# Two loads for expert 0's x, and b2 loaded behind the entry, in a mixture-of-experts kernel

## The chip, the cores and the metric

The kernel runs on one core of a Trainium2 chip. The metric is device time in microseconds (us); the median of three runs counts. All durations below come from one profiled execution.

## The reference

```python
# x (8, 256, 512), w1 (8, 512, 2048), w2 (8, 2048, 512), b1 (8, 2048), b2 (8, 512), all float32
h = np.matmul(x, w1) + b1[:, np.newaxis, :]
h = np.maximum(h, 0)
return (np.matmul(h, w2) + b2[:, np.newaxis, :]).astype(np.float32)
```

Eight experts, each with 256 rows of x: two matrix products, a bias and a ReLU between them, a bias behind. The weights are 64 MB of float32 in HBM, x and the output 4 MB each.

## The kernel before, in words

**Tiling.** All products are done in fp16 with float32 sums. An expert's first product makes h transposed, 128 of the 2048 hidden columns at a time: 16 groups j of four matmuls (128 x 128 weights against 128 x 256 of x transposed), summed in one of four PSUM tiles `ph`; ScalarE (ACT) adds b1 and applies the ReLU on the way into `hT` (L106). The second product sums over the 16 groups into `po`, 512 columns wide, in two halves of 128 rows, and begins with a matmul of one row of ones against b2 (L303). The results go over ACT or VectorE (DVE) into float32 tiles and from there to HBM.

**Steps.** TensorE (PE) runs a hardware loop of 11 steps (L268). In step s it does the first product of expert s (s < 8) and the second of expert s - 3. Before the first product it waits for `w1_in` and `xT_full` (L271, L272), before each half of the second for `w2_in` (L313). SyncE (SP) turns the completion of a weight load into `w1_in` or `w2_in`: in step s it waits for the load's semaphore `s_w1[s % 3]` (L144) and counts `w1_in` up; step 0 has no wait of its own.

**Weights.** Three buffers each for w1 and w2. GpSimd (POOL) issues the loads, which convert float32 to fp16 on the way (L163, L171): w1 of expert 0 ahead of everything (L352), w1 of experts 1 and 2 at once in `run_gpsimd`, and each later one when a buffer is free. w1 of expert 3 waits for `ph_full` = 16 (L162), that is until PE has done all 16 groups of expert 0. Each of these loads has 128 packets of 16 KB, 8 on each of the 16 DMA engines. All loads issued by POOL go through one DMA queue (q0, software), all issued by SP through another (q1, hardware).

**The start.** `first_loads` (L340) issues on SP: x of expert 0 and x of expert 1 (each 128 partitions of two rows, 4 KB in one piece, into `pair`), b1 (32 rows of 2 KB), and x of experts 2 and 3 together ("x2", 128 partitions of 8 KB, into `outg`). On POOL it issues w1 of expert 0 and then b2 (8 KB of fp16, one partition, 16 packets of 512 bytes). `first_turns` (L354) then makes an identity (POOL memsets, a DVE transpose at L360, ACT copies at L363), casts x of experts 0 and 1 to fp16 on ACT (L365), transposes them on PE (L372) and copies the result into `xT` on ACT (L373); DVE transposes b1 (L375), ahead of L360 in its order. A framework schedules these and inserts the waits.

**The entry.** Everything else stands in one critical section (L381) with semaphores written out by hand. On entry PE, ACT, DVE and SP each wait for every load and every engine of the start: the four loads of SP, w1 of expert 0, b2, and the last copies. POOL alone goes in without waiting and takes the same waits only at L180, after it has issued w1 of experts 1 and 2. Behind the entry ACT first counts `xT_full`, `ph_free` and the others up (L191 to L194) and casts x2 (L195), and DVE transposes it (L222).

**The end.** The groups' results leave on q0 (L187), the last two experts' on q1 (L155, L389).

Of the kernel before, what the change touches and what calls it, by code (L numbers as in the profile page):

```python
# [10 lines left out]
def kernel(  # L11
# [9 lines left out]
    nc = tc.nc  # L21
# [6 lines left out]
    nTB = T // P  # L28
# [5 lines left out]
    NW = 3  # L34
# [13 lines left out]
    def sb(name, shape, dt=fp16):  # L48
        return nc.alloc_sbuf_tensor(name, shape, dt).ap()

    w1_f = sb("w1sb", [P, NW * nKC * M + nJ])
    w1_sb = w1_f[:, 0 : NW * nKC * M].rearrange("p (n kc m) -> p n kc m", n=NW, kc=nKC)
# [6 lines left out]
    b2_sb = sb("b2sb", [1, E * H])  # L59
# [10 lines left out]
    def sem(name):  # L70
        return nc.alloc_semaphore(name)

    s_x = sem("s_x")
    s_w1 = [sem(f"s_w1_{i}") for i in range(NW)]
# [51 lines left out]
    def out_of(first, n):  # L126
        return out[first : first + n].rearrange("e (p r) h -> (e p) r h", r=n * nTB)

    x32 = {e: pair[e] for e in range(2)}
    x32[2] = grouped[0][:, 0 : FIRST[2] * nTB, :]  # L130

    def w1_of(e):
        return w1[e].rearrange("(p kc) m -> p kc m", kc=nKC)

    def x_of(first):
        n = FIRST[first]
        return x[first : first + n].rearrange("e (p r) h -> (e p) r h", r=n * nTB)

    def run_sync():
        s = nc.sync  # L140
        for step in range(E + LAG):
            if step < E:
                if step:
                    s.wait_ge(s_w1[step % NW], 16 * ((step + NW - 1) // NW))  # L144
                s.sem_inc(w1_in, 1)  # L145
            if step >= LAG:
                e = step - LAG
                for h in range(2):
                    if (e, h) in s_w2:
                        s.wait_ge(s_w2[e, h], 16)  # L150
                    s.sem_inc(w2_in, nQ // 2)  # L151
                    if e == E - 1 and h == 0:
                        s.wait_ge(po_free_a, E)
                        s.wait_ge(po_free_d, E)
                        s.dma_start(out=out_of(E - 2, 1), in_=pair[0]).then_inc(s_out[E - 2], 16)  # L155

    def run_gpsimd():
        g = nc.gpsimd

        def load_w1(e):  # L160
            if e >= NW:
                g.wait_ge(ph_full, nJ * (e - NW + 1))  # L162
            g.dma_start(out=w1_sb[:, e % NW], in_=w1_of(e)).then_inc(s_w1[e % NW], 16)  # L163

        def load_w2(e):
            if e >= NW:
                g.wait_ge(po_full, ENDS * (e - NW + 1))
            src = w2[e].rearrange("(p j) h -> p j h", j=nJ)
            cuts = (0, CUT[e], nJ) if e in CUT else (0, nJ)
            for h, (lo, hi) in enumerate(zip(cuts, cuts[1:])):  # L170
                g.dma_start(  # L171
                    out=w2_sb[:, e % NW, lo:hi], in_=src[:, lo:hi]).then_inc(s_w2[e, h], 16)

        for step in range(1, E + LAG):
            if step < E:
                if step == 4:
                    g.dma_start(out=x16[step], in_=x_of(step)).then_inc(s_x, 16)
                load_w1(step)
            if step == NW - 1:
                tc.wait_critical_data_deps()  # L180
            if step >= LAG:
                load_w2(step - LAG)
        g.wait_ge(s_w2[E - 1, 0], 16)
        for first in sorted(GROUPS, reverse=True):
            done = 1 + first + GROUPS[first]
            g.wait_ge(po_free_a, done)
            g.dma_start(out=out_of(first, GROUPS[first]), in_=grouped[first]).then_inc(  # L187
                s_out[first], 16)
# [150 lines left out]

    def first_loads():  # L340
        for to, rows in (
            (x32[0], x_of(0)),
            (x32[1], x_of(1)),
            (b1_rows, b1.rearrange("e (b i) -> (e b) i", b=nB)),
            (x32[2], x_of(2)),
        ):
            tc.keep_in_program_order(nc.sync.dma_start(out=to, in_=rows))  # L347
        for to, rows in (
            (w1_sb[:, 0], w1_of(0)),
            (b2_sb, b2.rearrange("e h -> (e h)").rearrange("(o f) -> o f", o=1)),  # L350
        ):
            tc.keep_in_program_order(nc.gpsimd.dma_start(out=to, in_=rows))  # L352

    def first_turns():  # L354
        g, v, a, t = nc.gpsimd, nc.vector, nc.scalar, nc.tensor
# [18 lines left out]
        for b in range(nB):  # L374
            v.transpose(  # L375
                out=b1T[b * B : (b + 1) * B, nB - 1 - b : nB - 1 - b + nJ * B],
                in_=b1_rows.rearrange("r (i j) -> r j i", j=nJ))

    first_loads()
    first_turns()  # L380
    with tc.tile_critical(sync_engine=mybir.EngineType.Pool, no_gpsimd_drain=True):  # L381
        run_gpsimd()
        run_sync()
        run_scalar()
        run_vector()
        run_tensor()
        nc.sync.wait_ge(po_free_a, 1 + E)
        nc.sync.wait_ge(po_free_d, 1 + E)
# [38 lines left out]
```

## Time and profile before

| | |
|---|---|
| median of 3 runs | 180.66 us (180.63 to 181.15) |
| profiled execution, its own time | 180.8 us |
| its span, first to last instruction | 179.0 us |
| mean granted TensorE clock | 0.975 |
| busy: PE, ACT, DVE, POOL | 73%, 48%, 21%, 7% of the span |
| DMA packets | 3825, 40.98 MB as counted at the destination |
| HBM read and written | 71.39 MB and 4.19 MB |

How to read the lines below. A line of the timeline has the start in us, the duration, the engine and the source line, the operation, the tile written and the one read, the count, and in brackets the idle time before it with what ended it; "SPq" and "POOLq" are the engines' own sequencers, which issue DMAs. A line of the DMA issues has the tile, the issuing engine, the count, the size as written in KB, and the median time from issue to landing. A line of the DMA queues has the queue, the number of its packets that started in the stretch, their MB, and the time that they took as a share of 16 engines. The "DMA" digits cut a stretch, or the whole span, into 40 equal slices and give in tenths how busy the 16 engines were. In a line of the waits stand who waited for whom, the total in us, the number of waits and the longest.

### The profile page before, as it was taken

How to read it: one execution, taken by the hardware profiler on the slowest of the kernel's cores; microseconds unless marked ns; L12 is line 12 of the kernel's file. 1: busy time of each engine (PE TensorE's matmuls, PEld its weight loads, DVE VectorE, ACT ScalarE, POOL GpSimd, SP SyncE). 2: the span in 40 equal slices, each digit the busy share in tenths (PEclk: the TensorE clock that was granted, in tenths of full speed). 3: DMA queues.
4: the chain of work that ended last, by engine and by line, in shares of the span. 5: the costliest groups of instructions: out<-in, count | busy, mean ns of one | idle time of the engine just before them, and what ended most of it. 6: DMA issues, size and time to landing. Idle time of an engine off the chain costs nothing.

```text
span 179.0 us, 2880 instructions
## 1 busy us (share of the span) xinstructions
PE 130.6 (73%) x800; PEld 86.5 (48%) x800; DVE 37.8 (21%) x39; ACT 86.3 (48%) x160; POOL 13.4 (7%) x30
## 2 busy tenths in 40 slices
PE   0004299596969993999956996699669997998940
PEld 0003278585858641786446644584268433443410
DVE  0092299300000299991000000000000000001010
ACT  3304658585858606674089705980398213121010
POOL 7100000302020101001010001000200001002000
PEclk9999999999999999579999999999999999999997
DMA  6999989999999998998999999899899999999995
GB/s 211 272 260 269 234 183 227 234 205 207 234 216 194 234 231 179 234 234 190 220 234 205 205 234 220 190 234 234 176 234 234 198 212 205 220 227 198 334 453 238
DMA packets 3825, 40.98 MB, mean 229 GB/s; under 512 B 448, under 2 KB 464, under 8 KB 1136
## 3 DMA queue, kind: packets, MB, share of 16 engines
q0 software_dynamic: 3056, 37.76, 95.2%
q1 hardware_dynamic: 768, 3.21, 4.6%
q14 instruction: 1, 0.01, 0.0%
HBM read 71.39 MB, written 4.19 MB: 422 GB/s over the span
## 4 chain that ended last, share of the span: by engine, by line
DMA 37%; PE 33%; ACT 16%; DVE 6%; issue 3%; SPq 1%; POOL 0%; ACTq 0%
PE po L318 18%; DMA w1sb<-in_w_dram 16%; PE ph L288 14%; DMA w2sb<-in_w_dram 11%; DMA outg<-in_x_dram 9%; ACT hTsb L106 8%; ACT outg L118 7%; DVE xTsb L222 6%; PE po L303 1%; ACT x L195 1%; SPq L347 1%; ACT pair L118 0%; POOL w2sb L171 0%; ACTq L422 0%; SPq L151 0%
## 5 line engine op out<-in xcount | busy, mean ns | idle before, releaser
L288 PE MATMUL ph<-xTsb,w1sb 128*128 x512 | 67.7, 291 | 23.0 <-SPq L145 7.8
L288 PEld LDWEIGHTS ph<-xTsb,w1sb 128*128 x512 | 58.5, 147 | 33.2 <-issue 30.5
L106 ACT ACTIVATE hTsb<-ph,b1T 128x256 f16<-128x256 f32 x128 | 56.8, 475 | 16.2 <-PE ph L288 15.7
L318 PE MATMUL po<-w2sb,hTsb 128*128 x256 | 56.8, 379 | 2.0 <-SPq L151 2.0
L118 ACT COPY outg<-po 32x1024 f32<-32x1024 f32 (+1 forms) x20 | 20.1, 1006 | 43.3 <-PE po L318 43.2
L318 PEld LDWEIGHTS po<-w2sb,hTsb 128*128 x256 | 24.9, 97 | 32.6 <-issue 5.1
L222 DVE STREAM_TRANSPOSE xTsb<-x 32x512 f16<-32x512 f16 (+1 forms) x32 | 31.0, 970 | 35.8 <-DMA x<-in_x_dram 28.5
L118 DVE COPY pair<-po 128x512 f32<-128x512 f32 x2 | 1.4, 692 | 88.2 <-PE po L318 88.2
L372 PE MATMUL ph<-ident,x 128*128 128x128 f16 x16 | 1.9, 310 | 15.7 <-ACT ident L363 15.7
L171 POOL DMA_DIRECT2D w2sb<-in_w_dram x10 | 5.3, 534 | 69.3 <-PE po L318 69.3
L372 PEld LDWEIGHTS <-x 128*128 128x128 f16 x16 | 1.6, 144 | 15.7 <-ACT ident L363 15.7
L163 POOL DMA_DIRECT2D w1sb<-in_w_dram x7 | 3.7, 536 | 65.8 <-PE ph L288 65.6
L118 ACT COPY pair<-po 128x512 f32<-128x512 f32 x2 | 1.2, 586 | 13.6 <-PE po L318 13.6
L375 DVE STREAM_TRANSPOSE b1T<-b1rows 32x512 f32<-32x512 f32 x4 | 4.1, 1023 | 9.3 <-DMA b1rows<-in_b_dram 9.2
L303 PE MATMUL po<-b2sb,ones 1*128 x16 | 4.8, 378 | 0.8 <-issue 0.7
L363 ACT COPY ident<-hTsb 32x32 f16<-32x32 f16 x4 | 1.0, 240 | 8.3 <-DVE hTsb L360 8.3
L365 ACT CAST x<-pair 128x1024 f16<-128x1024 f32 x2 | 2.1, 1044 | 2.3 <-DMA pair<-in_x_dram 2.3
L303 PEld LDWEIGHTS po<-b2sb,ones 1*128 1x128 f16 x16 | 1.4, 90 | 3.5 <-issue 3.2
L373 ACT COPY xTsb<-ph 128x1024 f16<-128x1024 f16 x2 | 1.9, 1014 | 1.1 <-PE ph L372 1.1
L195 ACT CAST x<-outg 128x2048 f16<-128x2048 f32 x1 | 1.9, 1900 | 0.8 <-DMA outg<-in_x_dram 0.8
L187 POOL DMA_DIRECT2D out_dram<-outg x2 | 1.1, 537 | 16.2 <-DMA w2sb<-in_w_dram 16.2
L365 ACT ACT_TABLE_LOAD x1 | 1.3, 1283 | 0.7 <-PEq L411 0.7
(12 smaller groups left out, 5.0 us busy)
## 6 DMA issues: line engine op xcount, KB each, us to landing
w1sb<-in_w_dram POOLq DMA_DIRECT2D x8, 2048.0 KB, 31.1
w2sb<-in_w_dram POOLq DMA_DIRECT2D x6, 2048.0 KB, 43.6
w2sb<-in_w_dram POOLq DMA_DIRECT2D x2, 1024.0 KB, 27.2
out_dram<-outg POOLq DMA_DIRECT2D x1, 2048.0 KB, 11.7
w2sb<-in_w_dram POOLq DMA_DIRECT2D x1, 1280.0 KB, 16.9
pair<-in_x_dram SPq DMA_DIRECT2D x2, 512.0 KB, 3.7
outg<-in_x_dram SPq DMA_DIRECT2D x1, 1024.0 KB, 16.8
x<-in_x_dram POOLq DMA_DIRECT2D x1, 1024.0 KB, 28.6
```

What stands on the lines that cost most here:

```text
L106: return nc.scalar.activation(out=to, in_=columns, func=relu_of, bias=b1T[:, at : at + 1], scale=1.0)
L118: return copy(out=t.rearrange("p (tb s) h -> p tb s h", s=split)[at : at + rows, lo:hi, k, :], in_=po[k * rows : (k + 1) * rows, e % 2, lo ...
L163: g.dma_start(out=w1_sb[:, e % NW], in_=w1_of(e)).then_inc(s_w1[e % NW], 16)
L171: g.dma_start(out=w2_sb[:, e % NW, lo:hi], in_=src[:, lo:hi]).then_inc(s_w2[e, h], 16)
L195: a.copy(out=x16[2], in_=x32[2]).then_inc(cast, 1)
L222: ins = v.transpose(out=to[b * B : (b + 1) * B, :, :, half * B : (half + 1) * B], in_=src.rearrange("p r (i kc) -> p kc r i", kc=nKC))
L288: ins = t.matmul(out=ph[i][:, 0:T], lhsT=w1_cols(w1_j, i, kc), rhs=x_cols[kc], start=(kc == 0), stop=(kc == nKC - 1),)
L303: t.matmul(out=po_f[:, bass.ds(o + tb * 512, H)], lhsT=ones1, rhs=b2_sb[0:1, bass.ds(b_e, H)], start=True, stop=False, skip_group_check=True,)
L318: ins = t.matmul(out=po_f[:, bass.ds(o + tb * 512, H)], lhsT=hT_f[:, bass.ds(h_e + (j * T + tb * P), P)], rhs=w2_f[:, bass.ds(w_e + j * H, ...
L365: a.copy(out=x16[e], in_=x32[e])
L372: t.transpose(out=to[:, kc, r, :], in_=rows[:, kc, :], identity=ident)
L375: v.transpose(out=b1T[b * B : (b + 1) * B, nB - 1 - b : nB - 1 - b + nJ * B], in_=b1_rows.rearrange("r (i j) -> r j i", j=nJ))
```

## The change

Three edits. x of expert 0 is loaded in two DMAs instead of one: its even rows (first half of each partition of `pair0`), then its odd rows, so 128 packets of 2 KB each instead of 128 of 4 KB. b2 leaves `first_loads`: POOL issues it inside the critical section, ahead of w1 of expert 1. Since b2 no longer belongs to the entry's waits, its completion counts on `s_w1[1]`, and SP waits for 16 more on that semaphore at the steps that use it (1, 4 and 7).

```diff
-                    s.wait_ge(s_w1[step % NW], 16 * ((step + NW - 1) // NW))
+                    s.wait_ge(s_w1[step % NW], 16 * ((step + NW - 1) // NW + (step % NW == 1)))
...
+        g.dma_start(
+            out=b2_sb, in_=b2.rearrange("e h -> (e h)").rearrange("(o f) -> o f", o=1),
+        ).then_inc(s_w1[1], 16)
         for step in range(1, E + LAG):
...
         for to, rows in (
-            (x32[0], x_of(0)),
+            *((x32[0][:, r], x_of(0)[:, r]) for r in range(nTB)),
             (x32[1], x_of(1)),
             (b1_rows, b1.rearrange("e (b i) -> (e b) i", b=nB)),
             (x32[2], x_of(2)),
         ):
             tc.keep_in_program_order(nc.sync.dma_start(out=to, in_=rows))
-        for to, rows in (
-            (w1_sb[:, 0], w1_of(0)),
-            (b2_sb, b2.rearrange("e h -> (e h)").rearrange("(o f) -> o f", o=1)),
-        ):
-            tc.keep_in_program_order(nc.gpsimd.dma_start(out=to, in_=rows))
+        tc.keep_in_program_order(nc.gpsimd.dma_start(out=w1_sb[:, 0], in_=w1_of(0)))
```

In the program as built, SP issues two loads of 128 x 512 into `pair0`, then expert 1's x, b1 and x2; POOL issues w1 of expert 0, the memsets, and behind its jump into the critical section b2 and w1 of experts 1 and 2. The entry waits for five SP loads instead of four, and no longer for b2. ACT's activation table load, its first instruction, takes over one of the two waits for x of expert 0. The order of work on every engine is otherwise as before.

## The prediction

> **What bounds the kernel now.** I read the page first, its DMA digits and queues.
>
> ```profile
> DMA  6999989999999998998999999899899999999995
> q0 software_dynamic: 3056, 37.76, 95.2%
> q1 hardware_dynamic: 768, 3.21, 4.6%
> w1sb<-in_w_dram POOLq DMA_DIRECT2D x8, 2048.0 KB, 31.1
> w2sb<-in_w_dram POOLq DMA_DIRECT2D x6, 2048.0 KB, 43.6
> w2sb<-in_w_dram POOLq DMA_DIRECT2D x1, 1280.0 KB, 16.9
> ```
>
> The 16 DMA engines are the bound: q0 (GpSimd's loads, above all the weights) and q1 (SP's loads and stores) together fill 99.8% of them. The time is therefore all packets laid end to end, plus every stretch in which the engines have nothing queued. Weights are issued long before they land (medians 31.1 and 43.6 us), so PE, ACT and DVE can be late without cost as long as POOL's next issue comes before the queue runs out. Next, the start, in the timeline.
>
> ```profile
> 0.74 0.86 SPq L347 DMA_DIRECT2D pair<-in_x_dram  x2
> 1.65 0.42 SPq L347 DMA_DIRECT2D b1rows<-in_b_dram  x1
> 2.12 0.42 SPq L347 DMA_DIRECT2D outg<-in_x_dram  x1
> 1.25 0.67 POOL L352 DMA_DIRECT2D w1sb<-in_w_dram  x1 [0.80 <-POOLq L411]
> 1.91 0.51 POOL L352 DMA_DIRECT2D b2sb<-in_b_dram  x1
> 3.97 1.09 POOL L163 DMA_DIRECT2D w1sb<-in_w_dram  x2 [0.16 <-issue]
> 21.11 10.26 PE L288 MATMUL ph<-xTsb,w1sb 128*128 x64 [3.50 <-issue]
> 31.67 0.53 POOL L163 DMA_DIRECT2D w1sb<-in_w_dram  x1 [26.61 <-PE ph L288]
> ```
>
> The link that matters is the last row: w1 of expert 3 is issued at 31.67, once PE has finished expert 0's 64 matmuls, which began at 21.11. Two more views: the chain of waits and the DMA issues (that of the second load at 3.97, then that of 31.67).
>
> ```profile
> 2.12 16.84 DMA outg<-in_x_dram
> w1sb<-in_w_dram POOLq DMA_DIRECT2D x1, 2048.0 KB, 32.6
> w1sb<-in_w_dram POOLq DMA_DIRECT2D x1, 2048.0 KB, 15.1
> ```
>
> PE begins 2.15 after x of experts 2 and 3 ("x2", tile outg) has landed at 2.12 + 16.84 = 18.96; that landing ends the entry of the critical section. The last weights queued before the entry (w1 of expert 2, issued at about 4.5) land at 4.5 + 32.6 = 37.1. So the issue at 31.67 is 5.4 us ahead of an empty queue. That is the thinnest cover of the kernel: the later loads named above land at least 16.9 us after issue, while the 1280 KB load, the quickest of them, needs some 6 us of engine time itself (five eighths of 8 packets of 1.21 us, worked out below).
>
> **The change, part by part.** First, how the two queues share the engines, from the DMA view cut to stretches: 0 to 4.65, 4.65 to 5.9 (two rows), 5.9 to 7.2 (two), 7.2 to 8.5 (two), 9.7 to 16 (two), 17.3 to 36.
>
> ```profile
> q1 hardware_dynamic: 265, 1.02, 61.6%
> ...
> q0 software_dynamic: 16, 0.26, 100.5%
> q1 hardware_dynamic: 23, 0.03, 6.3%
> ...
> q0 software_dynamic: 16, 0.26, 97.2%
> q1 hardware_dynamic: 16, 0.03, 8.0%
> ...
> q0 software_dynamic: 16, 0.26, 94.3%
> q1 hardware_dynamic: 16, 0.03, 7.4%
> ...
> q0 software_dynamic: 64, 1.05, 77.8%
> q1 hardware_dynamic: 73, 0.60, 23.3%
> ...
> q0 software_dynamic: 263, 4.05, 101.4%
> ```
>
> Up to 4.65 there are 265 packets of q1 and none of q0: x of experts 0 and 1, 8 packets of 4 KB each per engine, with completions. Then q0 enters with one packet on each of the 16 engines, then 16 packets of q1 (b1), 16 of q0, 16 of q1, and so on through x2: once both are queued, an engine takes one packet of each in turn. A w1 packet is dear: in the last row 263 packets, 16 of them mere completions, fill 18.7 us, which is 18.7 x 16 / 247 = 1.21 us each. A 2 KB packet took 7.4% x 1.3 us x 16 / 16 = 0.096 us, an 8 KB one 23.3% x 6.3 x 16 / 73 = 0.32. So any packet of q1 that arrives after w1's costs its queue 1.21 us of waiting.
>
> Why does q0 enter just behind expert 1's x, on all engines, though they finish it 0.3 us apart (4.65 to 5.0)? The digits of the first stretch (slices of 0.116 us), its first packets (1.70 to 1.83), and the stretches 165 to 167.4 and 167.4 to 168.3 of the tail, with the SP issue before them:
>
> ```profile
> DMA  0000000000000009442789899998899699979997
> q1 hardware_dynamic: 8, 0.03, 221.9%
> 164.48 0.34 SPq L155 DMA_DIRECT2D out_dram<-pair  x1
> q1 hardware_dynamic: 2, 0.01, 0.9%
> q1 hardware_dynamic: 75, 0.31, 84.1%
> ```
>
> SP's load issued at 0.74 starts in slice 15, at about 1.75: 1.0 us. In the tail the store issued at 164.48 gets 2 packets through before 167.4 and 75 after: it waits behind what the engines had already taken in, some 2 us of work. So engines take packets in by arrival, well ahead of moving them, and I read the start thus: w1's packets arrived after those of SP's second issue (1.18 + 1.0 = 2.2) and before those of its third (1.65 + 1.0 = 2.65), that is 0.95 to 1.4 us after POOL's issue at 1.25. The other reading, that w1 was ready only at about 4.1 and fell behind x by chance on 16 engines that end 0.3 us apart, I hold for much less likely.
>
> *The two loads of expert 0.* SP has one more issue, so its third, at 1.65, is now x of expert 1; b1 goes at about 2.12, x2 at about 2.58. POOL's first issue stays at 1.25. By my reading w1 now arrives ahead of expert 1's x, and nine more items of q1 per engine (8 packets, one completion) must alternate with q0. Counting turns: x2's completion is q1's 12th item behind w1's entry now, and the 12th of q0 is the first packet of w1 of expert 1 (8 of expert 0, its completion, b2 and its completion before it), 9 dear packets in all. As 21st it meets the 21st of q0: 8 + 8 + 1 = 17 dear packets. x2 lands 8 x 1.21 = 9.7 us later. Beside that, 16 packets of 2 KB replace 8 of 4 KB. One of 4 KB costs (stretch 2.6 to 4.6, 198 packets and 16 completions):
>
> ```profile
> q1 hardware_dynamic: 214, 0.81, 101.7%
> ```
>
> 101.7% x 2 x 16 / 198 = 0.16 us. So 16 x 0.096 - 8 x 0.16 = 0.26 us more engine time (0 if the 2 KB packet only costs its bytes, 0.08). This is on the bound and stays to the end: +0.26. x2 lands at 18.96 + 9.7 + 0.26 = 28.9. b1's completion meets the 12th item instead of the third, 6 dear packets later, so b1 lands at about 16.7; the rest of the entry chain:
>
> ```profile
> 9.22 4.13 DVE L375 STREAM_TRANSPOSE b1T<-b1rows 32x512 f32<-32x512 f32 x4 [9.22 <-DMA b1rows<-in_b_dram]
> 16.79 1.93 ACT L373 COPY xTsb<-ph 128x1024 f16<-128x1024 f16 x2 [1.13 <-PE ph L372]
> ```
>
> takes 18.72 - 9.2 = 9.5 us from b1 to the last transposed x and would end at 26.2, before x2. In the built program ACT's table load also waits for the second half of x0, and the casts stand behind it; x of expert 1 is in at 14.7 (x0's end at about 3.7, plus 8 x (1.21 + 0.16)), so all of this ends before or about when b1 lands, and b1's chain covers it.
>
> Entry, matmuls and POOL's issue all move by 9.9: w1 of expert 3 is issued at 31.67 + 9.9 = 41.6. Its data flow after the 0.95 to 1.4 us of arrival, value 1.2, plus a first packet's latency: 8 first packets took 221.9% x 0.13 x 16 / 8 = 0.58 us against 0.16, so 0.4. That is 43.2. When does the queue run dry? The digits of the stretch 36 to 37.2 (slices of 0.03 us) show where w1 of expert 2 ends and the next load starts:
>
> ```profile
> DMA  0000000000000000999990999909000000000000
> ```
>
> from 36.5 to 36.85, on the mean 36.65; with 0.26 more it is 36.9. Starved: 43.2 - 36.9 = 6.3 us. Bounds: arrival 0.95 and no latency, 5.6; if w1 of expert 0 was ready only when its first packet moved, 4.65 - 1.25 = 3.4, then 8.1. Nothing later makes this good, as the stream is gapless from there on. Nothing adds to it: every later issue keeps over 10 us of cover, and PE follows the stream, as its waits for weights show:
>
> ```profile
> PE ph L288 <- SPq L145: 7.8, 4, 3.2
> ```
>
> *b2 behind the entry.* In POOL's queue it moves behind the four memsets and still ahead of w1 of expert 1; in q0 it keeps its place between w1 of experts 0 and 1, the same packets. POOL's memsets come 0.5 earlier, its loads of 3.97 no earlier, as the b2 issue takes that 0.5. The waits of the entry, SP's view:
>
> ```profile
> SPq L422 <- DMA b2sb<-in_b_dram: 14.9, 1, 14.9
> SPq L422 <- DMA outg<-in_x_dram: 1.3, 1, 1.3
> ```
>
> b2 is late but x2 is 1.3 later still, so its removal from the entry buys nothing; at the other end, SP's wait for step 1 takes b2 along with w1 of expert 1, which is behind it in the same queue. 0, with no cover needed; bounds 0 and 0.
>
> Sum: 0.26 + 6.3 = 6.56 on the profiled execution's 180.8, 187.36; its own time stands 0.14 above the median 180.66, so **187.2**.
>
> *A rule against it.* The Trainium skill, "DMA: Bandwidth & Descriptors", Specifications, gives 0.6 us to the first byte for SP's loads and about 1 us for GpSimd's. By these, estimated, w1 would arrive at 2.25 and SP's third load at 2.25: a tie, and part of expert 1's x would slip in ahead, the in-between case below. The trace has 1.0 us for SP's load, and b1, third in SP's order, was behind w1 on every engine; I go by that.
>
> **The rivals.** (1) *Same order as before*: w1 is ready late and enters behind expert 1's x again. Then only the packets cost: 180.66 + 0.26 = 180.9 (180.7 at the low price). For it: the entry does coincide with the end of x. Against it: 16 engines of different ends.
>
> (2) *In between*: r of expert 1's 8 packets are left when w1 enters. x2 then comes (r + 1) x 1.21 + 0.26 later, and loss starts where issue, arrival and latency (31.67 + 1.2 + 0.4 = 33.3) pass 36.9, so from 3.6 us on, three turns. r = 1: 180.9; r = 4: 6.3 - 3.6 = 2.7, 183.6; r = 6: 8.7 - 3.6 = 5.1, 186.0. Same rows for and against.
>
> (3) *Faster*: the engines stand idle up to 1.75 and the first packets take 0.58 where 0.16 are moved. If a half load, with fewer bytes per packet, gets the engines going sooner, the whole stream moves up. Price: at most that latency of 0.4 and the half slice or so of the start, 0.5 in all, against the 0.26 of the packets; it decides only if w1 stays behind x. 180.4, and below 180.1 only with the 2 KB packet at the low price. Against it: the instruction issues as many packets as before at the same 0.74.
>
> (4) *The change doesn't do what it says*: the built program has two loads of 128 x 512 on SP and b2 behind POOL's entry jump, so only its effect on the entry fails, which I priced at 0.
>
> **How the numbers follow.** Likeliest case 0.60, at 187.2, its own range 186.5 (starved 5.6) to 189.0 (8.1). In between 0.14, 180.9 to 186.0. Same order 0.21, at 180.9. Faster mechanism 0.05, at 180.4. A measurement of this kernel can tell about 0.3% (0.54 us) from no change. The likeliest case alone holds 0.60, so the range takes in the in-between and the same-order cases down to 180.7: 180.7 to 189.0. Faster by over 0.3%: 0.03. Within: the same-order case nearly whole, and the rest of (3) and a small r, 0.23. Slower: 0.74.
>
> **What would show it.** In the changed profile: q0's first packet before about 4.0 us, ahead of 128 packets of expert 1's x that alternate with it; x of expert 1 landing near 14.7; b1 near 16.7; x2 near 28.9; PE's first matmul near 31; POOL's L163 issue near 41.6; and a hole of some 6 us in the DMA digits behind 37 (one or two of the 40 slices low). Wrong if x2 lands before 23, if the hole is missing, or if the DMA digits show a second hole.

## The result, and the profile after

The changed kernel takes 190.34 us (median of 6 runs, 189.65 to 191.28) against 180.69 us before (6 runs, 180.63 to 181.15): a ratio of 1.0531, with a 95% interval of 1.0510 to 1.0552. The forecast was 187.2 with a range up to 189.0, so the sign and the place of the loss were right and its size was not. The profiled execution took 191.28 us, the longest of the six, with a span of 189.5 us against 179.0. The ratios here and below leave out runs that lie over 1.5% above the fastest of their kernel, which concerns e5 and e7 alone.

The page of the changed kernel, its span, clock, DMA digits, queues and chain:

```profile
span 189.5 us, 2882 instructions
...
PEclk9999999999999999996999799987999699999998
DMA  7899999804999999999999999999999999999994
...
q0 software_dynamic: 3056, 37.76, 90.7%
q1 hardware_dynamic: 912, 3.21, 4.4%
...
PE 55%; ACT 22%; DMA 16%; issue 4%; SPq 1%; ACTq 0%
```

The bytes and q0's packets are the same as before, q1 has 144 more (912 against 768: 256 packets of 2 KB for 128 of 4 KB, and a load's 16 completions), and PE's clock is lowered in more slices (the digits under 9). What is new is one stretch near 40 us (slices 9 and 10 of 40, "0" and "4") in which the engines have nothing to do, called the hole below. "The stream" is all that the 16 DMA engines move, packet behind packet. The chain that ended last has changed hands: PE has 55% of it and DMA 16%. Of the kernel before the same line reads

```profile
DMA 37%; PE 33%; ACT 16%; DVE 6%; issue 3%; SPq 1%; POOL 0%; ACTq 0%
```

The timeline of the changed kernel, to be laid beside the rows that the prediction quotes (its lines are shifted: L350 is SP's loads, L351 w1 of expert 0, L174 b2, L291 the first product):

```profile
0.74 1.33 SPq L350 DMA_DIRECT2D pair<-in_x_dram  x3
1.25 0.67 POOL L351 DMA_DIRECT2D w1sb<-in_w_dram  x1 [0.80 <-POOLq L410]
...
2.12 0.43 SPq L350 DMA_DIRECT2D b1rows<-in_b_dram  x1
2.60 0.42 SPq L350 DMA_DIRECT2D outg<-in_x_dram  x1
...
3.52 0.50 POOL L174 DMA_DIRECT2D b2sb<-in_b_dram  x1 [0.20 <-issue]
4.00 1.10 POOL L163 DMA_DIRECT2D w1sb<-in_w_dram  x2
...
32.70 1.90 ACT L198 CAST x<-outg 128x2048 f16<-128x2048 f32 x1 [3.21 <-DMA outg<-in_x_dram]
...
34.27 9.51 PE L291 MATMUL ph<-xTsb,w1sb 128*128 x64 [5.88 <-issue]
...
44.07 0.53 POOL L163 DMA_DIRECT2D w1sb<-in_w_dram  x1 [38.97 <-PE ph L291]
```

All issues of the start are where the prediction had them. What lands is not: x of expert 1 at 17.92 (forecast 14.7), b1 at 19.97 (16.7), x2 at 32.16 (28.9). So PE begins 13.2 us later than before and w1 of expert 3 is issued 12.4 us later. The digits from 30 to 50 us, half a microsecond each, show what that leaves:

```profile
DMA  9999799997969914100000000000009910991909
```

From 37 to 39.5 one engine after the other runs dry, up to 45 none has work; counted from the packets, an engine is idle for 7.0 us on the mean between 35 and 45, and for 0.5 behind. Then, where did PE's cover go? PE's waits from 30 us on, changed kernel:

```profile
PE ph L291 <- issue: 13.1, 8, 5.9
PE ph L291 <- ACT hTsb L106: 10.6, 4, 2.7
PE po L306 <- issue: 0.9, 5, 0.2
```

In the kernel before, beside the waits for w1 that the prediction quotes (7.8 us), stand

```profile
PE ph L288 <- ACT hTsb L106: 4.9, 3, 2.0
...
PE po L318 <- SPq L151: 2.0, 3, 1.1
```

The waits for w1 and for w2 (L151) are gone, 9.8 us in all: no weight is late for PE any more, and ACT is waited for in their place. The end of the chain says the same, in time order (start, length, what). Before:

```profile
147.92 20.29 DMA w2sb<-in_w_dram
168.41 3.64 PE po L318 x16
```

After:

```profile
155.32 7.03 PE po L321 x32
162.88 7.01 PE po L321 x32
170.43 7.01 PE po L321 x32
177.98 7.03 PE po L321 x32
```

Before, the last load of w2 (768 KB of expert 7's) landed at 168.22 and PE, which had waited for it, had 16 matmuls (3.6 us) left to do. After, that load landed at 177.76, and PE, which came to it at 177.98 without a wait, block upon block, had 32 left (7 us).

### The profile page after: what moved, and what is told of

Same layout as the page of the kernel before. It is cut to its first block, busy times and chain, and to the rows that moved or that the text cites. A ratio compares the mean times of both kernels' runs of the same rounds, so it can differ in the third digit from the quotient of the medians.

```text
span 189.5 us, 2882 instructions
## 1 busy us (share of the span) xinstructions
PE 132.7 (70%) x800; PEld 88.4 (47%) x800; DVE 37.7 (20%) x39; ACT 86.3 (46%) x160; POOL 13.4 (7%) x30
## 4 chain that ended last, share of the span: by engine, by line
PE 55%; ACT 22%; DMA 16%; issue 4%; SPq 1%; ACTq 0%
PE po L321 30%; PE ph L291 23%; DMA outg<-in_x_dram 16%; ACT hTsb L106 13%; ACT outg L118 9%; PE po L306 2%; SPq L350 1%; ACT pair L118 0%; ACTq L421 0%; ACTq L197 0%; ACTq L196 0%; ACTq L195 0%; ACTq L194 0%
## 5 line engine op out<-in xcount | busy, mean ns | idle before, releaser
L291 PE MATMUL ph<-xTsb,w1sb 128*128 x512 | 70.1, 299 | 24.9 <-issue 13.1
L291 PEld LDWEIGHTS ph<-xTsb,w1sb 128*128 x512 | 60.3, 149 | 35.8 <-issue 32.1
L190 POOL DMA_DIRECT2D out_dram<-outg x2 | 1.1, 538 | 10.6 <-DMA w2sb<-in_w_dram 10.6
```

The source lines that it names most:

```text
L291: ins = t.matmul(out=ph[i][:, 0:T], lhsT=w1_cols(w1_j, i, kc), rhs=x_cols[kc], start=(kc == 0), stop=(kc == nKC - 1),)
```

## The experiments

**Theory**: w1's packets now arrive ahead of expert 1's x, each later packet of SP's queue waits 1.21 us for its turn, the entry is late, w1 of expert 3 is late. **Rivals**: 2 KB packets themselves are dear; b2's new place costs; the number of SP loads, not what is in them, decides. Then, for the 3 us beyond the forecast: PE has become a bound of its own, or the stream has lost more than the hole, or both. "Landing" below is the completion of a load's slowest engine, "first matmul" that of PE's first product.

### e1: the split alone

```diff
-            (x32[0], x_of(0)),
+            *((x32[0][:, r], x_of(0)[:, r]) for r in range(nTB)),
```

> Expert 0's x in two loads, b2 left where it was. Theory (turns: SP's third load, now x of expert 1, arrives behind w1 of expert 0 and alternates with it): the whole loss is here, 189 to 191.5 us, x2 landing near 32. Rival (b2: its move, with POOL's memsets right behind the first w1 issue, delays w1's start or step 1): 180.7 to 181.2, x2 landing near 19. Rival (packets of 2 KB are what costs): as the theory, so the next runs must tell these two apart.

Measured: 190.55 us (189.83 to 191.08), ratio 1.0548 [1.0522, 1.0575]. x2 lands at 30.86, first matmul 33.01, w1 of expert 3 issued at 43.13, idle 7.1. The split is the whole loss.

### e2: b2's move alone

```diff
+        g.dma_start(
+            out=b2_sb, in_=b2.rearrange("e h -> (e h)").rearrange("(o f) -> o f", o=1),
+        ).then_inc(s_w1[1], 16)
...
-            (b2_sb, b2.rearrange("e h -> (e h)").rearrange("(o f) -> o f", o=1)),
```

> b2 behind the entry, expert 0's x in one load. Turns: nothing, 180.4 to 181.0, x2 landing near 19. Rival b2: most of the loss, 185 to 190.

Measured: 180.73 us (180.63 to 181.25), ratio 0.9997 [0.9983, 1.0012]. With b2 on `s_w1[1]` and SP's waits as in the change, its place is worth nothing, as forecast (x2 lands at 20.22 in its profile, 1.3 us later than before, and that costs nothing either).

### e3: two loads of 64 partitions, in 4 KB packets

```diff
-            (x32[0], x_of(0)),
+            *((x32[0][h : h + 64], x_of(0)[h : h + 64]) for h in (0, 64)),
```

> Two loads for expert 0's x, but of 64 partitions each, so the packets stay at 4 KB and their number at 128. Turns: SP's third load is again x of expert 1, so 187 to 191, x of expert 1 landing above 14, x2 above 27. Rival packets: 180.5 to 181, x2 landing near 19.

Measured: 195.06 us (194.16 to 195.51), ratio 1.0782 [1.0741, 1.0824]. No packet has changed its size, and the loss is larger, above the expected band. The timeline tells why:

```profile
0.74 1.81 SPq L347 DMA_DIRECT2D pair<-in_x_dram  x3
1.25 0.67 POOL L352 DMA_DIRECT2D w1sb<-in_w_dram  x1 [0.80 <-POOLq L411]
...
2.60 0.43 SPq L347 DMA_DIRECT2D b1rows<-in_b_dram  x1
```

Three issues take 1.81 us, 0.6 each, instead of 1.33 in the changed kernel; now even expert 0's second half arrives behind w1 (it lands at 10.96), then x of expert 1 at 19.62 and x2 at 35.63. So the loss needs no 2 KB packets; it goes with the order of arrival.

### e4: one load of 2 KB packets

```diff
-    x32 = {e: pair[e] for e in range(2)}
+    x32 = {0: grouped[4][:, 0:3:2, :], 1: pair[1]}
```

The tile's two rows lie apart, so each partition needs two packets of 2 KB, in one instruction.

> One load for expert 0's x, with 256 packets of 2 KB: its two rows go to places 4 KB apart. Turns: x of expert 1 stays SP's second load, so only the packets' own time shows: 180.7 to 181.1, x2 landing 19.0 to 20. Rival packets: 186 or more.

Measured: 188.07 us (187.4 to 188.33), ratio 1.0395 [1.0363, 1.0428]: the expectation missed. The timeline:

```profile
0.74 0.64 SPq L347 DMA_DIRECT2D outg<-in_x_dram  x1
1.25 0.67 POOL L352 DMA_DIRECT2D w1sb<-in_w_dram  x1 [0.80 <-POOLq L411]
1.44 0.57 SPq L347 DMA_DIRECT2D pair<-in_x_dram  x1
...
31.27 10.14 PE L288 MATMUL ph<-xTsb,w1sb 128*128 x64 [5.91 <-issue]
41.70 0.53 POOL L163 DMA_DIRECT2D w1sb<-in_w_dram  x1 [36.63 <-PE ph L288]
```

256 packets take 0.64 us to issue, so x of expert 1 goes out at 1.44 instead of 1.18, and that is late enough: it lands at 15.93, x2 at 29.12. The run was meant to leave the order alone and instead brackets it: w1, issued at 1.25, is behind a second SP load of 1.18 and ahead of one of 1.44 (the first load's own packets also begin 0.4 us later here, at 2.16). It also does what was forecast for the changed kernel nearly to the digit (x2 29.12, first matmul 31.27, issue 41.70, idle 6.1 us): the count of turns is right where all engines do as counted.

### e5: w1 of expert 0 issued 0.67 us later, in the changed kernel

```diff
-        tc.keep_in_program_order(nc.gpsimd.dma_start(out=w1_sb[:, 0], in_=w1_of(0)))
...
+        for tile_, value in ((steps, 0.0), (ident, 0.0), (ones1, 1.0)):
+            tc.keep_in_program_order(g.memset(tile_, value))
+        tc.keep_in_program_order(g.dma_start(out=w1_sb[:, 0], in_=w1_of(0)))
```

> The changed kernel, with w1 of expert 0 issued behind three of POOL's four memsets instead of ahead of them, so some 1.2 us later. Theory (turns, by order of arrival): x of expert 1 and b1 are in before w1, and the whole loss goes: 180.5 to 181.3, x of expert 1 landing near 5.5, x2 before 20. Rival (the number of loads or the 2 KB packets cost by themselves, whatever arrives first): 187 or more stays.

Measured: four runs of 182.15, 183.87, 188.63 and 189.00 us (of the lower two the ratio is 1.0113 [1.0043, 1.0184]). Neither expectation came true. POOL's memsets begin earlier without the load ahead of them, so the delay is small, from 1.25 to 1.92:

```profile
1.92 0.67 POOL L356 DMA_DIRECT2D w1sb<-in_w_dram  x1
...
2.12 0.43 SPq L350 DMA_DIRECT2D b1rows<-in_b_dram  x1
```

This is a dead heat with SP's third load, issued at 1.65: x of expert 1 completes on some engines at 5.2 us and on others at 17.5, as if each had decided for itself, and the time changes by 7 us from run to run. That is the in-between case of the prediction, one edit away from the kernel measured, and it shows that the loss hangs on w1's arrival against SP's third load.

### e6: the kernel before, with b1 second and x of expert 1 third

> The kernel before, with b1 as SP's second load and x of expert 1 as its third; no split, no small packets of x, b2 as before. Turns: the third load is behind w1 again: x of expert 1 lands above 13, x2 above 27, 186 to 192. Rival (the split or the packets): 180.5 to 181.2, x2 near 19.

Measured: 185.39 us (184.83 to 186.13), ratio 1.0258 [1.0217, 1.03]. No load is split; expert 1's x is only third instead of second. It lands at 16.11, x2 at 27.0, and

```profile
1.18 0.42 SPq L347 DMA_DIRECT2D b1rows<-in_b_dram  x1
1.25 0.67 POOL L352 DMA_DIRECT2D w1sb<-in_w_dram  x1 [0.80 <-POOLq L411]
1.66 0.41 SPq L347 DMA_DIRECT2D pair<-in_x_dram  x1
...
29.14 9.12 PE L288 MATMUL ph<-xTsb,w1sb 128*128 x64 [9.12 <-SPq L145]
38.56 0.53 POOL L163 DMA_DIRECT2D w1sb<-in_w_dram  x1 [33.51 <-PE ph L288]
```

The mechanism without the change. It comes out 0.6 us below the expected band, since b1's three items are ahead of w1 here: as its 18th item x2's completion meets two w1 packets fewer, 28.9 - 0.26 - 2.4 = 26.2 by the count, and the engines complete it between 26.08 and 27.0.

### e7, e8, e9: which bound holds the 190 us

e7 takes the hole away: w2 of expert 0 is issued ahead of w1 of expert 3, so that the queue has work. e8 takes PE's work away instead. e9 does both.

```diff
 e7, e9:
+            if step == LAG:
+                load_w2(0)
...
-            if step >= LAG:
+            if step > LAG:
 e8, e9:
-                        for j in range(QJ):
+                        for j in range(QJ // 2):
```

> The changed kernel, with w2 of expert 0 issued ahead of w1 of expert 3 and so right behind the entry, near 32, while the stream still has w1 of expert 2 to move. Both theories: the hole of the DMA engines behind 38 goes. Theory stream (the prediction's: the hole is what costs): 181 to 184. Rival PE (the work of PE and ACT from the entry on takes 157 us of itself, so that a late entry costs whatever the DMA does): 189.5 to 191.5, as the changed kernel.

> The changed kernel, of whose second product each half sums 4 of its 8 groups, so half of that sum is left out and PE has some 28 us less to do; all loads stay. The hole stays. Stream alone: 189 to 190.5, about the changed kernel's time less a late tail. PE alone, with no part for the stream: 181 to 184.

> The changed kernel with both edits of the two runs before: w2 of expert 0 ahead of w1 of expert 3, and half of each sum of the second product left out. If hole and PE's own length are two bounds side by side, each enough for the loss, taking away both gives the time of the stream alone: 180.5 to 182.5, though x2 still lands near 31. If something third binds (the order of the packets, the entry itself): above 185.

Measured, with the changed kernel for comparison:

| | second product whole | second product halved |
|---|---|---|
| with the hole | 190.34 (189.65 to 191.28) | e8: 190.76 (189.38 to 191.22), ratio 1.055 [1.0508, 1.0592] |
| hole filled | e7: 190.30 (189.04, 190.30, 191.07; a fourth run 194.34), ratio 1.0507 [1.0445, 1.0569] | e9: 183.20 (182.90 to 183.52), ratio 1.0132 [1.0115, 1.0149] |

Either cure alone gives nothing, both together give 7.1 us. (e8 lies 0.3 above the first of its two bands.) The page of e7 is that of its longest run, 194.34 us, in which two engines moved even the second half of expert 0's x behind w1 (they complete it at 9.76 and 10.95, the others by 4.41), so that x2 lands at 35.57 and PE begins at 37.71. How long that run took says nothing on the cure; its digits show the hole of 40 us gone:

```profile
DMA  7999999998999999999999999999999995399962
```

The engines idle late instead (slices 34 and 35, 5.6 us between 159 and 169), because buffers come free only as PE gets through: the last two loads of w2 are issued at 165.71 and 166.23, when the load before them has landed at 162.58. e8's chain, on the other hand, ends on the stream again:

```profile
153.30 23.54 DMA w2sb<-in_w_dram
177.03 1.91 PE po L321 x8
```

So the changed kernel has two bounds of nearly the same length. The stream's last weights land 10.8 us before the span ends, the outputs behind them, in the kernel before (168.22 of 179.0) as in e8 (176.84 of 187.6) and, within 0.1, in e4, e6, e9, e10 and e15; by that the changed kernel's stream, at 177.76, asks for 188.5. PE takes 154.3 to 154.9 us from its first matmul to the end where no hole is in its way (e11 and e7, table below), and 34.27 + 154.3 to 154.9 is 188.6 to 189.2. e9 missed its expected band by 0.7 at the top: without hole and without PE's load 2.5 us stay. Its page has no low slice, but w1 of expert 2 completes between 37.36 and 40.08 on the 16 engines, where the kernel before has 36.8 to 37.1: that is the start, of which more below.

### e10, e11: the late entry without any change of order

In the kernel before, ACT waits for w1 of expert 1 before it lets PE begin (e10); e11 also fills the hole as in e7.

```diff
+        a.wait_ge(s_w1[1], 16)
```

> The kernel before, its loads untouched; ACT waits for w1 of expert 1 (it lands at 27.4) before it counts the entry's semaphores up, so PE starts 8.5 us later and nothing else changes at the start. Both theories of a late entry: PE, 27.4 + 157 + 1.8 = 186.2 (185 to 187.3); stream, issue of w1 of expert 3 at 40.2, hole 5.1, 185.8. Rival (the order of the packets costs by itself): 180.5 to 181.5.

> The late entry again, with w2 of expert 0 issued ahead of w1 of expert 3, so that the stream has no hole. PE: 185 to 187.3, as without. Stream: 180.5 to 182.

Measured: e10 185.15 us (184.63 to 185.61), ratio 1.0254 [1.0232, 1.0277]; e11 184.95 us (183.56 to 185.28), ratio 1.0221 [1.0171, 1.027]. All loads of the start land as before or within 1 us of it (x2 at 19.13 and 19.97), only PE is late. In e10:

```profile
28.81 9.37 PE L289 MATMUL ph<-xTsb,w1sb 128*128 x64 [11.09 <-ACTq L195]
38.48 0.53 POOL L163 DMA_DIRECT2D w1sb<-in_w_dram  x1 [33.43 <-PE ph L289]
```

7.7 us of delay cost 4.5, with an idle stretch of 3.3 us (e10) and without one (e11: its chain is PE's to the end, and its last weights land 11.9 us before the end, not 10.8). e10 by itself would not tell: its stream asks for the same time (last weights at 172.06, 10.8 before the end). e11 does: a late entry alone costs, and a full queue does not mend it.

### e12: w1 of expert 0 last

```diff
-            (w1_sb[:, 0], w1_of(0)),
...
+        spare = hT[:, NH - 1, nJ // 2 :, :]
+        for tile_, value in ((steps, 0.0), (ident, 0.0), (ones1, 1.0), (spare, 0.0)):
+            tc.keep_in_program_order(g.memset(tile_, value))
+        tc.keep_in_program_order(g.dma_start(out=w1_sb[:, 0], in_=w1_of(0)))
```

> The kernel before, with w1 of expert 0 issued behind b2 and four memsets (one of them of an unused place, for delay), so that all of SP's loads are in before w1. x2 lands near 7.5, the entry ends near 15 with b1's chain instead of 18.96, PE starts 4 us sooner. Stream bound: no gain, 180.3 to 181.2. If the entry is on the path of the kernel before: 176.5 to 179.

Measured: 181.79 us (181.63 to 181.97), ratio 1.0063 [1.0046, 1.008]. With w1 issued at 4.81 all of SP's loads run ahead and x2 lands at 8.95, but I had overlooked that the entry also waits for w1 of expert 0, which lands at 18.61:

```profile
4.81 0.55 POOL L358 DMA_DIRECT2D w1sb<-in_w_dram  x1
...
19.46 1.90 ACT L195 CAST x<-outg 128x2048 f16<-128x2048 f32 x1 [3.38 <-DMA w1sb<-in_w_dram]
21.19 9.44 PE L288 MATMUL ph<-xTsb,w1sb 128*128 x64 [6.22 <-issue]
```

PE begins when it did before, so the run, above the first of its two bands, says nothing on an early entry. The 1.1 us that it loses (0.9 between the two profiles) lie in the stream: the engines idle 0.4 us between 5 and 10, and the last w2 lands at 169.08, 0.9 later than before.

### e13, e14, e15: why x2 lands 2 to 3 us behind the count

e13 splits expert 1's x instead of expert 0's, e14 is e1 with b1 as SP's third load and expert 1's x as its fourth, e15 is the changed kernel once more.

```diff
 e13:
-            (x32[1], x_of(1)),
+            *((x32[1][:, r], x_of(1)[:, r]) for r in range(nTB)),
 e14 (beside e1's split):
-            (x32[1], x_of(1)),
             (b1_rows, b1.rearrange("e (b i) -> (e b) i", b=nB)),
+            (x32[1], x_of(1)),
```

> The kernel before with expert 1's x, not expert 0's, in two loads of 2 KB packets: even rows in SP's second issue, odd rows in its third. By the turns, the odd rows (third issue, 1.65) fall behind w1 of expert 0 and x2's completion is again nine items later: x2 lands at 28.9 at the least, PE begins near 31, w1 of expert 3 is issued near 41.6, time 187 to 190.5. What it tells apart is the extra 2 to 3 us of the changed kernel. If w1's first packets are slow because too little of x stands ahead of them (here x of expert 0 and half of expert 1's, some 2.05 us of packets, not 1.54), they are hidden and x2 lands at 28.5 to 29.5, with w1 of expert 2 complete on all engines within 0.6 us. If they are slow because of a third SP load that arrives with them, x2 lands at 30.5 to 32.5 and the completions spread by 2 us or more. Rival to the whole: only splitting expert 0's x matters, as it is the first load; then the time stays at 180.7 to 181.2.

> The changed kernel's split alone (b2 as before), with b1 as SP's third issue and x of expert 1 as its fourth. The count of items behind w1 is the same, so by the turns x2 lands near 28.9 plus whatever w1's first packets take too long. If these are slow because the 128 packets of expert 1's x arrive with them, x2 lands at 28.5 to 29.8, w1 of expert 2's completions lie within 0.8 us, time 187 to 188.5. If they are slow because two loads of 2 KB packets stand ahead of them, x2 lands at 30.5 to 32.5, the completions spread by 2 us or more, time 189.5 to 191.5.

> The changed kernel once more, for a second profile of it. If the slow first packets of w1 belong to the kernel, x2 lands again at 31.5 to 32.5 and w1 of expert 2's completions spread by 2 us or more; if the first profile was one draw of several, x2 lands anywhere from 29 to 35 and the time follows it by no more than 1 us for each.

Measured (two runs each): e13 189.90 us, ratio 1.0491 [1.0428, 1.0553]; e14 191.31 us, ratio 1.0569 [1.0526, 1.0612]; e15 189.84 us, ratio 1.0487 [1.0425, 1.0549]. The DMA view of the stretch 3.1 to 5.06 gives the first packets of w1 (packets, MB, share of 16 engines). Changed kernel:

```profile
q0 software_dynamic: 16, 0.26, 104.0%
```

e15:

```profile
q0 software_dynamic: 22, 0.36, 102.3%
```

e14:

```profile
q0 software_dynamic: 16, 0.26, 100.2%
```

e4:

```profile
q0 software_dynamic: 18, 0.29, 72.7%
```

e13, from 4.4 to 6.7, as w1 enters later there:

```profile
q0 software_dynamic: 31, 0.51, 110.2%
```

One packet took share x stretch x 16 / packets: 2.04 us, 1.46, 1.96, 1.27 and 1.31, where the kernel before has 1.2 to 1.3 on the mean. In e14 it isn't expert 1's x that arrives with w1, and the packets are as slow; e14's x2 lands at 32.20. In e4, with the same bytes ahead of w1 in one load, they are not. So the slow packets go with two loads of 2 KB packets ahead of w1 in these five. But they are not confined to them. e3, with no 2 KB packet ahead of w1, has for its first 16 (3.1 to 4.6 us)

```profile
q0 software_dynamic: 16, 0.26, 102.7%
```

that is 1.54 us each, and in the changed kernel the first 16 packets of w1 of expert 3, behind the hole and with nothing small ahead of them (45 to 47 us), have

```profile
q0 software_dynamic: 16, 0.26, 98.1%
```

1.96 us each; in every kernel with a hole these take 1.8 to 2.0, and the ones behind them 1.23. At the start they are slow (1.5 to 2.0 for the first 16) in every kernel whose w1 begins to move before 3.5 us, and 1.25 to 1.4 in those where it begins from 3.6 on, so that this reading fits as well; no run tells the two apart. e13 fell between my two expectations: its packets are hardly slow, yet x2 lands at 30.99, and w1 of expert 2 completes within 1.24 us, one packet. Expert 1's first half lands between 4.50 and 5.42 there while w1's packets begin between 4.53 and 5.15: on some engines w1 may have been in while a write of that half was still to come, and these would count one turn more. e15's x2 lands at 31.40, so the 32.16 is within a microsecond of what the kernel does.

## Why the prediction was right and wrong

**The bound before, right.** The thinnest cover was w1 of expert 3, and it is where the hole opened, in every late kernel (e1, e3, e4, e6, e10).

**The reading of the start, right.** Arrival decides: a second SP load of 1.18 is ahead of w1 (on all engines but two in e7's profile), one of 1.44 behind it (e4), any third load behind it (e1, e6), and a w1 issued 0.67 later ties with the third (e5). The other reading, w1 ready only at 4.1, is out: in the changed kernel it moves packets at 3.3. The tie that the Trainium skill's first-byte figures ("DMA: Bandwidth & Descriptors", Specifications) would make of 1.25 against 1.65 did not come about.

**The count of turns, right.** x2's completion as the 21st item gave 28.9. The 16 engines complete x2 between 29.07 and 32.16 in the changed kernel, 28.92 and 30.86 in e1, 28.72 and 31.40 in e15, 28.78 and 29.12 in e4.

**The failing step: "x2 lands at 18.96 + 9.7 + 0.26 = 28.9".** That is the fastest engine, and a load has landed when its slowest engine is done, here at 32.16. The count took every w1 packet at 1.21 us and all engines alike. Before, with all of expert 1's x ahead of w1, that holds: the first 16 packets took 1.26 on the mean and the engines lie 0.3 us apart. In the changed kernel the first 16 took 2.04 on the mean, up to 2.64, and the engines lie 2.4 us apart when w1 of expert 0 lands and 3.1 when x2 does. The term was mis-sized by 3.3 us. It went on to PE's first matmul (34.27, forecast 31), and, as expert 0's product took 9.51 instead of 10.26, with 2.5 us to the issue of w1 of expert 3 (44.07, forecast 41.6). The 6.3 us forecast were 5.9 of idle engines and 0.4 of a first packet's latency. Measured are 7.5 of idle engines, less than 5.9 + 2.5 because the same slow engines ran dry some 1 us later, and 0.74 on each engine by which the first packets behind the hole took longer than 1.23: 8.2 in all. The arrival in that sum was right: the first packet moves at 45.30, 1.23 after the issue.

**A second one: "Nothing adds to it".** The stream lost more than the hole. Its last weights land 9.54 us later (177.76 against 168.22): 7.5 idle in the hole and 0.74 by its first packets, 0.46 more idle between the first packet, at about 1.75, and 5 us (0.60 against 0.14), and 0.85 more on each engine for w1 packets before the hole that took longer than 1.23. That is 9.55. The 0.26 for the 2 KB packets does not show: 16 of them took 16 x 0.098 = 1.57 us where 8 of 4 KB had taken 8 x 0.183 = 1.46 (means of all 256), 0.1 more, and all of q1's packets up to 40 us took 0.04 more per engine. e9 is the run that shows the start's part bare: 2.5 us with neither hole nor PE in the way. The cover of "over 10 us" shrank as well, without opening a second hole: the last two loads of w2 are issued from 162.65 on, 5.3 before the load ahead of them lands at 167.93.

**And: "PE follows the stream".** Before it did, with 9.8 us of waits for weights. But those waits were not slack in full. From PE's first matmul to the end of the span:

| kernel | first matmul | to the end |
|---|---|---|
| before | 21.11 | 157.9 |
| e10, e11 (late entry) | 28.81, 28.59 | 154.0, 154.3 |
| e6 (b1 second) | 29.14 | 153.9 |
| e4 (one load) | 31.27 | 154.9 |
| e1 (split alone), e15 | 33.01, 33.50 | 154.8, 154.2 |
| changed | 34.27 | 155.2 |
| e3 (by partition) | 37.78 | 155.1 |
| e7 (hole filled) | 37.71 | 154.9 |
| e8 (half of the second product) | 33.61 | 154.0 |

The column alone does not show a bound of PE's. Where there is a hole, the rest of the stream begins with the issue of w1 of expert 3, which follows PE's first matmul by about 10 us, so the stream too keeps its length from there; e8, with PE busy for 111.1 us instead of 132.7, has 154.0 like the others. The rows that show the bound are e11 and e7, which have no hole: 154.3 and 154.9. However late PE begins, it can by these make up about 3 us, not 10, as waits for ACT (10.6 us instead of 4.9) and a lower granted clock (0.94 from 60 to 180 us, 0.97 before from 47 to 168, by the windows) come in their place. So beyond 3 us a late entry costs its full length on PE too, whatever the queue does (e7, e11). In the changed kernel this bound lies 0 to 1 us above the stream's, by the time from the last weights to the end: 177.76 + 10.8 = 188.5 of a span of 189.5 in the one profile, 176.92 + 10.8 = 187.7 of 187.7 in the other (e15). That the forecast from the stream alone came within 3.1 us rests on the two being nearly equal here.

The profiled execution, the longest of the six, grew by 10.5 us in its span where 6.6 were forecast. The 4.0 between them are 1.9 from the hole, 0.5 and 0.85 from the start and 1.0 from PE, less some 0.2 that the 2 KB packets did not cost. In e15, whose span grew by 8.7, the 2.1 are 1.5, 0.2, 0.5 and nothing from PE, less the same 0.2. The 3.1 us by which the medians miss lie between.

**b2, right**: 0 (e2). **Rivals**: same order and faster are out. In between is real, but belongs to e5. The range ended at 189.0 because its upper end priced only w1's readiness; no step put a price on engines that differ from each other.

**Left open**: why w1's first packets take 2 us and more on some engines, at the start of the changed kernel and behind every hole, and not in e4; and how first packets that are 0.8 us slower on the mean leave the engines 3 us apart (in e3, whose first ones took 1.54 us each, they are 0.6 apart).

## What to carry to other kernels

An extra DMA at the head of a queue is not its own 0.4 us: every load behind it arrives 0.4 us later, and if that puts one behind a load of large packets on another queue, each of its packets waits a large packet's time. Count landings by the slowest engine, not by the mean or the fastest. And when a stage that feeds two resources becomes late, price both, the stream's empty stretch and the compute engine's remaining length, since curing one alone (e7, e8) may show nothing.

## What the runs showed of the hardware

- Issuing a load on SP took 0.39 to 0.43 us for 128 packets over 128 partitions, but 0.64 for 256 packets (e4) and 0.55 to 0.58 for 64 packets over 64 partitions (e3). The first packet of SP's first load came 1.0 us after the issue began, but 1.3 in e3 and 1.4 in e4.
- A third SP load seems to take some 0.2 us longer to arrive than a second: expert 1's x as second load, issued at 1.18, is ahead of a w1 issued 0.07 later on all engines (before); as third, at 1.65, it only ties with a w1 issued 0.27 later (e5). This takes w1's own way to be as long in both, which no run shows.
- The two queues alternated by single packets, 16 KB of the one against 2, 4 or 8 KB of the other: 16 of the one, 16 of the other over the 16 engines. Which load meets which was set here by a few tenths of a microsecond of arrival (e4, SP's second issue at 1.44 instead of 1.18), worth 7 us at the end.
- The first 16 packets of 16 KB behind a stretch of idle engines took 1.8 to 2.0 us on the mean in every kernel with a hole, those behind them 1.23.
